# A hybrid attention block in float32: conv projections from unnormed rows, attention moved behind them, norm steps on VectorE, joined weight splits

## The chip, the cores and the metric

The kernel runs on one core of a Trainium2 chip. The metric is the device time of one execution in microseconds. One execution was taken by the hardware profiler; the rows below are of that one. TensorE (PE) multiplies matrices and loads its stationary operand beside that (PEld); VectorE (DVE), ScalarE (ACT) and GpSimd (POOL) work on elements; SyncE (SP) starts most DMA transfers.

## The reference

A layer with four token mixers side by side, merged by gates, and a feed-forward part, for 512 tokens of 1024 channels:

```python
# x: 1 x 512 x 1024, float32; one layer
h = rms_norm(x, attn_norm)                       # x * rsqrt(mean(x^2) + 1e-6) * gain
proj = einsum('bsd,dc->bsc', h, w_in)            # split into 17 parts:
(fq, fk, fv, ff, cu, cb, cc, mq, mk, mv, mi, mf, mo, sq, sk, sv, gates) = split(proj)

fq, fk = rms_norm(fq per head, fox_q_gain), rms_norm(fk per head, fox_k_gain)
# forget-gate attention, 4 heads of 64, causal, softmax over
#   q.k/8 + c_q - c_k   with c = cumsum(log_sigmoid(ff + bias))
y_fox = fox_attention(fq, fk, fv, ff + fox_f_bias)

def short_conv_mixer(u, b_gate, c_gate, w):
    z = c_gate * u
    y = conv over 3 positions of the sequence, one weight per channel and tap
    return b_gate * y
y_conv = short_conv_mixer(cu, cb, cc, conv_w)    # 256 channels

y_mlstm = sigmoid(mo) * rms_norm(mlstm(mq, mk, mv, mi, mf), mlstm_h_gain)
y_swa = swa_attention(rms_norm(sq), rms_norm(sk), sv, sinks, bias)   # 8 heads, window 128

g = sigmoid(gates)                               # 4 x 1024
merged = (g0 * (y_fox @ w_fox_out) + g1 * (y_conv @ w_conv_out)
        + g2 * (y_mlstm @ w_mlstm_out) + g3 * (y_swa @ w_swa_out))
x = x + merged @ w_merge_out
h = rms_norm(x, ffn_norm)
x = x + (silu(h @ w_gate) * (h @ w_up)) @ w_down      # 1024 -> 2816 -> 1024
```

## The kernel before

Everything lies transposed: channels on the 128 partitions, the 512 tokens along a row, so x is eight blocks of 128 x 512. TensorE works on a rounded float type (F32R); so each float32 operand is split into a high half, a cast made by ScalarE, and a low half, the difference, made by VectorE (`split`, lines 132 to 134; `scaled_split`, 136 to 139, with a factor per channel). A product is three matmuls in `mm3`: high with high (line 128), high with low and low with high.

**Weights** stream in through SP's queue in 139 pieces of 512 KB, each 1024 columns wide. `w_split` (line 160) splits half a piece, 512 columns, at a time; `w_take` hands them out and keeps `w_ahead` (5) halves split ahead; `w_raw` (3) pieces and `w_buf` (9) split halves have buffers.

**Start** (from line 222). For each of the eight blocks xc: the product with the channel gain is split into xh and xl (the list `xg`, rows that the norm has not touched), a token-major projection of 396 columns runs (psn, with weights wnr split into wnh, wnl of 396 columns each), and the squares go into `ssq`, added on GpSimd (line 243). From ssq come `rcol` and `rb_` (r = 1/sqrt(mean + eps), one value per token, spread over all partitions by a matmul with ones, pv_a), and `epsv`.

**Projections.** `proj` (line 394) multiplies eight blocks with two weight halves: 24 matmuls of 128 x 512. pfk and pfq (two each) use xg, since a norm per head follows them. The conv's pcu, pcc and pcb (two each), and every gate and projection behind them, use `xn`: `normed_input` (line 384) loads a block of x again as xs, multiplies it with rb_ on GpSimd (line 387) and splits it into xnh, xnl.

**Norm per head** (`head_normed`, `sum_split`, `head_normed_rest`, lines 438 to 465): ScalarE squares the projection, the square is split into u (cast on VectorE, line 447) and w (difference, on GpSimd, line 448), a matmul with `blk` sums over the head, VectorE and ScalarE make the inverse root (`rsqrt`, 141 to 146), GpSimd multiplies (line 464), then `k_stack` or `q_stack` split the result. It serves fk and fq (each twice), sk and sq0 to sq3.

**The conv** (lines 689 to 706): z = pcc x pcu, two shifted additions, times pcb, split into ych, ycl. **The gates** (`gated`, line 711): for each of eight output blocks d a projection of 24 matmuls with xn (gconv0 to gconv7), then the branch's out-projection (oconv), tanh on ScalarE, and VectorE multiplies and adds up.

**Order.** Each mm3 of a projection calls `tick()`. It counts down work that was put off by `later(steps, ...)`; each `period` ticks, if nothing is put off, it lets one step of a background generator run. Such generators are `fox_attention` (22 steps), `swa_attention` and `ml_attention`. `gate_rows` (line 310), in five steps, makes the gate rows, writes them to memory and reads four of them back, spread over all partitions, as negc (line 305, ScalarE's queue), for fox_attention's scores. `flush()` runs all that is left. In program order fox_attention begins when the first pcc is done, and is flushed behind `gated("conv")`; then come psk and psq0 to psq3, then `gated("fox")`. The framework's scheduler may then move an instruction ahead of others on its engine.

Of the kernel before, what the change touches and what calls it, by code (L numbers as in the profile page):

```python
# [8 lines left out]
F32 = mybir.dt.float32  # L9
# [7 lines left out]
P = 128  # L17
# [20 lines left out]
    "n_s": 58, "n_wk": 11, "w_raw": 3, "w_buf": 9, "w_ahead": 5, "mm": 4,  # L38
    "norm_lag": 18, "fox_p": 6, "fox_t": 4, "fox_v": 6, "swa_p": 10, "swa_t": 3, "swa_v": 5, "swa_d": 0,
    "ml_p": 4, "ml_v": 3, "ml_n": 8, "warm": 7, "xn_0": 3, "xn_p": 3,  # L40
# [4 lines left out]
def kernel(  # L45
# [114 lines left out]
    def w_split():  # L160
        i = stream["split"]
        if i >= 2 * n_w:
            return
        stream["split"] = i + 1
        while stream["raw"] <= min(i // 2 + W_RAW - 1, n_w - 1):
            w_load()
        raw = stream["raws"][i // 2][:, (i % 2) * NT:(i % 2) * NT + NT]
        hi = big.tile([P, NT], F32R, tag="whi", name=f"wh{i}", bufs=W_BUF)
        lo = big.tile([P, NT], F32R, tag="wlo", name=f"wl{i}", bufs=W_BUF)
        split(hi, lo, raw)  # L170
        stream["ready"].append((hi, lo))

    def w_take():
        while len(stream["ready"]) <= W_AHEAD and stream["split"] < 2 * n_w:
            w_split()
        return stream["ready"].pop(0)
# [7 lines left out]
    pace = {"period": 4, "count": 0}  # L184
# [12 lines left out]
    def tick():  # L197
        for d in deferred:
            d[0] -= 1
        due = [d for d in deferred if d[0] <= 0]  # L200
        for d in due:
            deferred.remove(d)
            d[1]()
        pace["count"] += 1
        if pace["count"] >= pace["period"] and not deferred:
            pace["count"] = 0
            bg()
# [19 lines left out]
    for ko in range(KO):  # L227
# [4 lines left out]
        wh = big.tile([P, NV], F32R, tag="whi", name=f"wnh{ko}", bufs=W_BUF)  # L232
        wl = big.tile([P, NV], F32R, tag="wlo", name=f"wnl{ko}", bufs=W_BUF)
        split(wh, wl, wr[ko // 2][:, (ko % 2) * NV:(ko % 2) * NV + NV])
# [3 lines left out]
        if ko == 0:  # L238
            nc.scalar.activation(ssq, xc[ko], AF.Square)
        else:  # L240
            sq = wk(f"xsq{ko}")
            nc.scalar.activation(sq, xc[ko], AF.Square)
            nc.gpsimd.tensor_tensor(ssq, ssq, sq, op=ALU.add)

    rb_ = s_tile("r_b")
    epsv = s_tile("epsv")
    rcol = const.tile([P, NB], F32, name="rcol")
# [21 lines left out]
    norm_rows(ssq, rb_, epsv, "a")  # L269

# [37 lines left out]
    def gate_rows():  # L308
# [19 lines left out]
        for hh in range(FOX_H):  # L328
            negc.append(bcast_row(f"negc{hh}", hh))
# [54 lines left out]
    def normed_input(ko):  # L384
        t = wk(f"xs{ko}")
        nc.sync.dma_start(t, xT[ko * P:(ko + 1) * P, :])
        nc.gpsimd.tensor_tensor(t, t, rb_, op=ALU.mult)
        h, l = s_tile(f"xnh{ko}", F32R), s_tile(f"xnl{ko}", F32R)
        scaled_split(h, l, t, col[:, C_AN + ko:C_AN + ko + 1])
# [55 lines left out]
    def sum_split(name, sq):  # L445
        h, l = s_tile(f"{name}u", F32R), s_tile(f"{name}w", F32R)
        nc.vector.tensor_copy(h, sq)
        nc.gpsimd.tensor_tensor(l, sq, h.bitcast(F32), op=ALU.subtract)
        return h, l
# [5 lines left out]
    def head_normed_rest(name, qg, sq, s2, eps, then):  # L455
# [8 lines left out]
        nc.gpsimd.tensor_tensor(qg, qg, sq, op=ALU.mult)  # L464
# [17 lines left out]
    def fox_attention():  # L482
        prob, trans, outs, sums = {}, {}, {}, {}

# [191 lines left out]
    for n in (6, 14, 22, 30, 38):  # L676
        later(n, lambda: next(gr, None))
    later(40, lambda: next(bl, None))
# [9 lines left out]
    for p in range(2):  # L688
        ps = proj(f"pcu{p}")
        u = wk(f"cu{p}")  # L690
        nc.scalar.copy(u, ps)
        ps = proj(f"pcc{p}")
        z = wk(f"cz{p}")
        nc.vector.tensor_tensor(z, ps, u, op=ALU.mult)
        if p == 0:
            pace["period"] = TUNE["fox_p"]
            background.append(fox_attention())
# [4 lines left out]
        ps = proj(f"pcb{p}")  # L702
# [36 lines left out]

    gated("conv", False)  # L740
    flush()
# [9 lines left out]

    gated("fox", False, TUNE["swa_p"], swa_attention)
# [207 lines left out]
```

## Time and profile before

| | before |
|---|---|
| median of 3 runs (lowest, highest) | 863.8 us (862.32, 864.12) |
| the profiled execution, and its span | 862.88 us, 861.1 us |
| TensorE busy, matmuls | 846.6 us (98%), x3879 |
| VectorE busy | 493.4 us (57%), x899 |
| ScalarE busy | 386.1 us (45%), x733 |
| GpSimd busy | 144.9 us (17%), x134 |
| mean DMA rate over the span | 101 GB/s |

Busy time is the time in which an engine worked on an instruction, as a share of the span. A matmul that follows another overlaps with it, so a row's duration (0.39 us) is longer than the distance between two starts (0.23 us). The granted clock (PEclk) is TensorE's clock as a share of full speed, 1.00 being 2.4 GHz.

### The profile page before, as it was taken

The numbers are of one execution on the slowest core, as the hardware profiler recorded it, in microseconds if no ns is written. First come the engines' busy times: TensorE is split into PE (matmuls) and PEld (weight loads), VectorE is DVE, ScalarE is ACT, GpSimd is POOL, SyncE is SP. The second block draws the span as 40 slices with busy tenths as digits, with TensorE's granted clock in tenths as the row PEclk, the third lists the DMA queues.
The fourth block names the chain that finished last, engine by engine and source line by source line (L and its number), as shares of the span: only waits on it lengthen the run. The fifth ranks groups of instructions, "written<-read, shape, count | busy, mean of one in ns | idle before, by whom it ended". The sixth has DMA issues, their size and how long they took to land.

```text
span 861.1 us, 10668 instructions
## 1 busy us (share of the span) xinstructions
PE 846.6 (98%) x3879; PEld 699.6 (81%) x3879; DVE 493.4 (57%) x899; ACT 386.1 (45%) x733; POOL 144.9 (17%) x134
## 2 busy tenths in 40 slices
PE   7999999999999999999999999999999999999998
PEld 6877788888788888888888888888888888888886
DVE  6899966459888886675745545444444333522320
ACT  7565555467665654554534444333333322322210
POOL 5262100024312001221211202111111111000000
PEclk9998999999999999999999999999999999999999
DMA  6642222242221522222224423222222232233310
GB/s 232 214 136 97 87 74 74 96 125 73 74 74 50 172 83 88 75 74 98 98 98 141 150 78 120 94 99 89 97 94 96 97 99 97 97 123 110 123 37 24
DMA packets 28520, 87.35 MB, mean 101 GB/s; under 512 B 3455, under 2 KB 5032, under 8 KB 28468
## 3 DMA queue, kind: packets, MB, share of 16 engines
q1 hardware_dynamic: 24716, 80.87, 27.6%
q10 hardware_dynamic: 3752, 5.81, 2.3%
q8 instruction: 30, 0.49, 0.2%
q14 instruction: 22, 0.18, 0.1%
HBM read 84.53 MB, written 2.13 MB: 101 GB/s over the span
## 4 chain that ended last, share of the span: by engine, by line
PE 84%; DVE 8%; ACT 3%; issue 2%; DMA 2%; SPq 0%; POOL 0%; DVEq 0%; ACTq 0%; POOLq 0%
PE dn L130 5%; PE fu L128 5%; PE dn L129 5%; PE fg L128 5%; PE fu L130 5%; PE fg L130 5%; PE fu L129 5%; PE fg L129 5%; PE dn L128 5%; PE gswa L129 2%; PE gswa L128 2%; PE gswa L130 2%; PE gmlstm L128 2%; PE gmlstm L130 2%; PE mg L130 2%
## 5 line engine op out<-in xcount | busy, mean ns | idle before, releaser
L134 DVE TENSOR_TENSOR wl<-wr,wh 128x512 fp32r<-128x512 f32 x278 | 203.0, 733 | 154.9 <-ACT wh L133 153.6
L133 ACT CAST wh<-wr 128x512 fp32r<-128x512 f32 x278 | 170.4, 619 | 262.7 <-PE dn L129 69.1
L823 POOL TENSOR_TENSOR ut<-ut,gt 128x512 f32<-128x512 f32 x22 | 34.2, 1554 | 204.8 <-DVE ut L822 166.6
L129 PE MATMUL fu<-x2l,wh 128*128 128x512 f32 x176 | 68.5, 389 | 0.0
L128 PE MATMUL fu<-x2h,wh 128*128 128x512 f32 x176 | 68.5, 389 | 0.0
L130 PE MATMUL fg<-x2h,wl 128*128 128x512 f32 x176 | 68.5, 389 | 0.0
L130 PE MATMUL fu<-x2h,wl 128*128 128x512 f32 x176 | 68.5, 389 | 0.0
L128 PE MATMUL fg<-x2h,wh 128*128 128x512 f32 x176 | 68.5, 389 | 0.0
L129 PE MATMUL fg<-x2l,wh 128*128 128x512 f32 x176 | 68.5, 389 | 0.0
L128 PE MATMUL dn<-ah,wh 128*128 128x512 f32 x176 | 68.5, 389 | 0.0
L129 PE MATMUL dn<-al,wh 128*128 128x512 f32 x176 | 68.5, 389 | 0.0
L130 PE MATMUL dn<-ah,wl 128*128 128x512 f32 x176 | 68.5, 389 | 0.0
L130 PEld LDWEIGHTS fg<-x2h,wl 128*128 128x128 f32 x176 | 33.1, 188 | 6.9
L129 PEld LDWEIGHTS fu<-x2l,wh 128*128 128x128 f32 x176 | 33.1, 188 | 6.9
L128 PEld LDWEIGHTS dn<-ah,wh 128*128 128x128 f32 x176 | 33.0, 188 | 6.9
L129 PEld LDWEIGHTS dn<-al,wh 128*128 128x128 f32 x176 | 33.0, 188 | 6.9
L129 PEld LDWEIGHTS fg<-x2l,wh 128*128 128x128 f32 x176 | 33.0, 188 | 6.9
L128 PEld LDWEIGHTS fu<-x2h,wh 128*128 128x128 f32 x176 | 33.1, 188 | 6.8
L130 PEld LDWEIGHTS fu<-x2h,wl 128*128 128x128 f32 x176 | 33.0, 187 | 6.9
L130 PEld LDWEIGHTS dn<-ah,wl 128*128 128x128 f32 x176 | 33.0, 188 | 6.7
L128 PEld LDWEIGHTS fg<-x2h,wh 128*128 128x128 f32 x176 | 33.0, 188 | 6.7
L822 DVE TENSOR_TENSOR ut<-fu,r 128x512 f32<-128x512 f32 x22 | 15.2, 691 | 29.9 <-PE fu L130 29.9
(598 smaller groups left out, 1930.7 us busy)
## 6 DMA issues: line engine op xcount, KB each, us to landing
wr<-in_w_str_dram SPq DMA_DIRECT2D x139, 512.0 KB, 3.3
xc<-in_xT_dram SPq DMA_DIRECT2D x8, 256.0 KB, 5.5
xs<-in_xT_dram SPq DMA_DIRECT2D x8, 256.0 KB, 4.0
xr<-in_xT_dram ACTq DMA_DIRECT2D x8, 256.0 KB, 2.6
out_dram<-o SPq DMA_DIRECT2D x7, 256.0 KB, 2.1
wnr<-in_w_tok_dram SPq DMA_DIRECT2D x3, 396.0 KB, 5.6
negc<-d_rows ACTq DMA_DIRECT2D x4, 256.0 KB, 5.7
bw<-d_line ACTq DMA_DIRECT2D x4, 256.0 KB, 3.7
```

What stands on the lines that cost most here:

```text
L128: nc.tensor.matmul(out, a[0], b[0], start=start, stop=False)
L129: nc.tensor.matmul(out, a[0], b[1], start=False, stop=False)
L130: nc.tensor.matmul(out, a[1], b[0], start=False, stop=stop)
L133: nc.scalar.copy(hi, src)
L134: nc.vector.tensor_tensor(lo, src, hi.bitcast(F32), op=ALU.subtract)
L822: nc.vector.tensor_tensor(ut, pu, r2, op=ALU.mult)
L823: nc.gpsimd.tensor_tensor(ut, ut, gt, op=ALU.mult)
```

## The change

- **Weights** are split 1024 columns at a time, one cast and one subtraction for a whole piece: 139 splits in place of 278. There are 4 buffers of 1024 columns for each half in place of 9 of 512, 4 in place of 3 raw pieces, and the look-ahead is 4 halves. At the start, pairs of 396 columns are split together (792), but for the first pair.
- **From GpSimd to VectorE** go the seven additions into ssq, the low halves in `sum_split`, the multiplication in `head_normed_rest`, and the one in `normed_input`, which now also takes the channel gain in, so that a plain split follows.
- **The conv projections** use xg. Since pcu and pcc are linear in the row, their product needs r twice: ScalarE makes r_sq = r x r, VectorE multiplies pcu by it in place of ScalarE's copy, and multiplies the conv's result with rb_ ahead of the product with pcb.
- **Later steps.** The first `normed_input` runs at tick 26, then one each 6 ticks (3 and 3 before); gate_rows at 8, 18, 28, 40, 50 (6 to 38 before).
- **fox_attention** is put into the background behind the conv projections and a flush, with period 5 (6 before), and runs on through psk and psq, where put-off work no longer holds it back (`mixed`). The negc loads stand at its beginning. A flush stands ahead of `gated("fox")`.

```diff
--- before.py
+++ after.py
@@ -35,9 +35,9 @@
 
 
 TUNE = {
-    "n_s": 58, "n_wk": 11, "w_raw": 3, "w_buf": 9, "w_ahead": 5, "mm": 4,
-    "norm_lag": 18, "fox_p": 6, "fox_t": 4, "fox_v": 6, "swa_p": 10, "swa_t": 3, "swa_v": 5, "swa_d": 0,
-    "ml_p": 4, "ml_v": 3, "ml_n": 8, "warm": 7, "xn_0": 3, "xn_p": 3,
+    "n_s": 58, "n_wk": 11, "w_raw": 4, "w_buf": 4, "w_ahead": 4, "mm": 4,
+    "norm_lag": 18, "fox_p": 5, "fox_t": 4, "fox_v": 6, "swa_p": 10, "swa_t": 3, "swa_v": 5, "swa_d": 0,
+    "ml_p": 4, "ml_v": 3, "ml_n": 8, "warm": 7, "xn_0": 26, "xn_p": 6,
 }
 
 
@@ -159,19 +159,19 @@
 
     def w_split():
         i = stream["split"]
-        if i >= 2 * n_w:
+        if i >= n_w:
             return
         stream["split"] = i + 1
-        while stream["raw"] <= min(i // 2 + W_RAW - 1, n_w - 1):
+        while stream["raw"] <= min(i + W_RAW - 1, n_w - 1):
             w_load()
-        raw = stream["raws"][i // 2][:, (i % 2) * NT:(i % 2) * NT + NT]
-        hi = big.tile([P, NT], F32R, tag="whi", name=f"wh{i}", bufs=W_BUF)
-        lo = big.tile([P, NT], F32R, tag="wlo", name=f"wl{i}", bufs=W_BUF)
-        split(hi, lo, raw)
-        stream["ready"].append((hi, lo))
+        hi = big.tile([P, 2 * NT], F32R, tag="whi", name=f"wh{i}", bufs=W_BUF)
+        lo = big.tile([P, 2 * NT], F32R, tag="wlo", name=f"wl{i}", bufs=W_BUF)
+        split(hi, lo, stream["raws"][i])
+        for h in (slice(0, NT), slice(NT, 2 * NT)):
+            stream["ready"].append((hi[:, h], lo[:, h]))
 
     def w_take():
-        while len(stream["ready"]) <= W_AHEAD and stream["split"] < 2 * n_w:
+        while len(stream["ready"]) <= W_AHEAD and stream["split"] < n_w:
             w_split()
         return stream["ready"].pop(0)
 
@@ -181,7 +181,7 @@
 
 
     background, deferred = [], []
-    pace = {"period": 4, "count": 0}
+    pace = {"period": 4, "count": 0, "mixed": False}
 
     def later(steps, fn):
         deferred.append([steps, fn])
@@ -202,7 +202,7 @@
             deferred.remove(d)
             d[1]()
         pace["count"] += 1
-        if pace["count"] >= pace["period"] and not deferred:
+        if pace["count"] >= pace["period"] and (pace["mixed"] or not deferred):
             pace["count"] = 0
             bg()
 
@@ -229,9 +229,15 @@
         xh, xl = s_tile(f"xh{ko}", F32R), s_tile(f"xl{ko}", F32R)
         scaled_split(xh, xl, xc[ko], g)
         xg.append((xh, xl))
-        wh = big.tile([P, NV], F32R, tag="whi", name=f"wnh{ko}", bufs=W_BUF)
-        wl = big.tile([P, NV], F32R, tag="wlo", name=f"wnl{ko}", bufs=W_BUF)
-        split(wh, wl, wr[ko // 2][:, (ko % 2) * NV:(ko % 2) * NV + NV])
+        half = slice((ko % 2) * NV, (ko % 2) * NV + NV)
+        if ko % 2 == 0:
+            wnh = big.tile([P, 2 * NV], F32R, tag="whi", name=f"wnh{ko}", bufs=W_BUF)
+            wnl = big.tile([P, 2 * NV], F32R, tag="wlo", name=f"wnl{ko}", bufs=W_BUF)
+            if ko:
+                split(wnh, wnl, wr[ko // 2])
+        if ko < 2:
+            split(wnh[:, half], wnl[:, half], wr[0][:, half])
+        wh, wl = wnh[:, half], wnl[:, half]
         for t in range(NB):
             tb = slice(t * P, (t + 1) * P)
             mm3(ps_n[t][:, 0:NV], (xh[:, tb], xl[:, tb]), (wh, wl), ko == 0, ko == KO - 1)
@@ -240,10 +246,11 @@
         else:
             sq = wk(f"xsq{ko}")
             nc.scalar.activation(sq, xc[ko], AF.Square)
-            nc.gpsimd.tensor_tensor(ssq, ssq, sq, op=ALU.add)
+            nc.vector.tensor_tensor(ssq, ssq, sq, op=ALU.add)
 
     rb_ = s_tile("r_b")
     epsv = s_tile("epsv")
+    r_sq = s_tile("r_sq")
     rcol = const.tile([P, NB], F32, name="rcol")
 
     def norm_rows(ssq, r_out, epsv_out, tag):
@@ -267,6 +274,7 @@
     nc.vector.tensor_scalar(vc, pcv[:, :, 0], 1.0 / D, EPS, op0=ALU.mult, op1=ALU.add)
     rsqrt(vc, rcol, yc, tcl)
     norm_rows(ssq, rb_, epsv, "a")
+    nc.scalar.activation(r_sq, rb_, AF.Square)
 
     snk = const.tile([P, SWA_H], F32, name="snk")
     nc.sync.dma_start(snk, bass.AP(sinks.tensor, sinks.offset, [[0, P], [1, SWA_H]]))
@@ -325,8 +333,6 @@
         nc.vector.tensor_tensor_scan(c[0:64], on[0:64], a[0:64], 0.0, op0=ALU.mult, op1=ALU.add)
         nc.vector.tensor_scalar(a[0:4], c[0:4], -1.0, None, op0=ALU.mult)
         nc.scalar.dma_start(d_rows[0:4], a[0:4])
-        for hh in range(FOX_H):
-            negc.append(bcast_row(f"negc{hh}", hh))
         yield
         ai = wk("g_ai")
         nc.gpsimd.memset(ai[0:64], 0.0)
@@ -384,9 +390,10 @@
     def normed_input(ko):
         t = wk(f"xs{ko}")
         nc.sync.dma_start(t, xT[ko * P:(ko + 1) * P, :])
-        nc.gpsimd.tensor_tensor(t, t, rb_, op=ALU.mult)
+        nc.vector.scalar_tensor_tensor(
+            t, t, col[:, C_AN + ko:C_AN + ko + 1], rb_, op0=ALU.mult, op1=ALU.mult)
         h, l = s_tile(f"xnh{ko}", F32R), s_tile(f"xnl{ko}", F32R)
-        scaled_split(h, l, t, col[:, C_AN + ko:C_AN + ko + 1])
+        split(h, l, t)
         xn.append((h, l))
 
 
@@ -445,7 +452,7 @@
     def sum_split(name, sq):
         h, l = s_tile(f"{name}u", F32R), s_tile(f"{name}w", F32R)
         nc.vector.tensor_copy(h, sq)
-        nc.gpsimd.tensor_tensor(l, sq, h.bitcast(F32), op=ALU.subtract)
+        nc.vector.tensor_tensor(l, sq, h.bitcast(F32), op=ALU.subtract)
         return h, l
 
     def head_sums(pm, s2):
@@ -461,7 +468,7 @@
         else:
             nc.vector.scalar_tensor_tensor(v, pm, 1.0 / HD, eps, op0=ALU.mult, op1=ALU.add)
         rsqrt(v, sq, y0, sq)
-        nc.gpsimd.tensor_tensor(qg, qg, sq, op=ALU.mult)
+        nc.vector.tensor_tensor(qg, qg, sq, op=ALU.mult)
         then(qg)
 
 
@@ -481,6 +488,8 @@
 
     def fox_attention():
         prob, trans, outs, sums = {}, {}, {}, {}
+        for hh in range(FOX_H):
+            negc.append(bcast_row(f"negc{hh}", hh))
 
         def scores(h, qt):
             q2, (ka, kb) = fq[h // 2][h % 2], fk[h // 2][h % 2]
@@ -673,9 +682,9 @@
     y["fox"], y["conv"], y["swa"], y["mlstm"] = [], [], [], []
     fq, fk, sq_, sk, mq, mk, mo, vm = [], [], [], [], [], [], [], []
     gr, bl = gate_rows(), swa_bias_line()
-    for n in (6, 14, 22, 30, 38):
+    for n in (8, 18, 28, 40, 50):
         later(n, lambda: next(gr, None))
-    later(40, lambda: next(bl, None))
+    later(56, lambda: next(bl, None))
     for ko in range(KO):
         later(TUNE["xn_0"] + TUNE["xn_p"] * ko, lambda ko=ko: normed_input(ko))
     for p in range(2):
@@ -686,20 +695,19 @@
 
 
     for p in range(2):
-        ps = proj(f"pcu{p}")
+
+        ps = proj(f"pcu{p}", xg)
         u = wk(f"cu{p}")
-        nc.scalar.copy(u, ps)
-        ps = proj(f"pcc{p}")
+        nc.vector.tensor_tensor(u, ps, r_sq, op=ALU.mult)
+        ps = proj(f"pcc{p}", xg)
         z = wk(f"cz{p}")
         nc.vector.tensor_tensor(z, ps, u, op=ALU.mult)
-        if p == 0:
-            pace["period"] = TUNE["fox_p"]
-            background.append(fox_attention())
         cw = [col[:, C_CW + 2 * k + p:C_CW + 2 * k + p + 1] for k in range(3)]
         nc.scalar.activation(u, z, AF.Copy, scale=cw[2])
         nc.vector.scalar_tensor_tensor(u[:, 1:], z[:, :-1], cw[1], u[:, 1:], op0=ALU.mult, op1=ALU.add)
         nc.vector.scalar_tensor_tensor(u[:, 2:], z[:, :-2], cw[0], u[:, 2:], op0=ALU.mult, op1=ALU.add)
-        ps = proj(f"pcb{p}")
+        nc.vector.tensor_tensor(u, u, rb_, op=ALU.mult)
+        ps = proj(f"pcb{p}", xg)
         nc.vector.tensor_tensor(u, ps, u, op=ALU.mult)
         yh, yl = s_tile(f"ych{p}", F32R), s_tile(f"ycl{p}", F32R)
         split(yh, yl, u)
@@ -737,8 +745,11 @@
                 pace["period"] = period
                 background.append(then())
 
+    flush()
+    pace["period"] = TUNE["fox_p"]
+    background.append(fox_attention())
     gated("conv", False)
-    flush()
+    pace["mixed"] = True
 
 
     swa_bias_load()
@@ -749,6 +760,8 @@
         ps = proj(f"psq{p}")
         head_normed(f"sq{p}", ps, qgain[:, 1:2], None, lambda q, p=p: sq_.append(q_stack(f"sq{p}", q, falling=True)))
 
+    pace["mixed"] = False
+    flush()
     gated("fox", False, TUNE["swa_p"], swa_attention)
```

The order on each engine, with the numbers of the program's buffers. First VectorE in the start, where the low halves xl of the input blocks stand among weight splits. Before:

```order
L134 TENSOR_TENSOR wnl_252<-wnr_84,wnh_251 128x396
L138 SCALAR_TENSOR_TENSOR xl_225<-xc_82,col,xh_224 128x512
L134 TENSOR_TENSOR wnl_275<-wnr_90,wnh_274 128x396
L134 TENSOR_TENSOR wnl_298<-wnr_90,wnh_297 128x396
L138 SCALAR_TENSOR_TENSOR xl_248<-xc_86,col,xh_247 128x512
```

and after:

```order
L138 SCALAR_TENSOR_TENSOR xl_219<-xc_82,col,xh_218 128x512
L249 TENSOR_TENSOR ssq<-ssq,xsq_257 128x512
L134 TENSOR_TENSOR wnl_265<-wnr_90,wnh_264 128x792
L249 TENSOR_TENSOR ssq<-ssq,xsq_280 128x512
L138 SCALAR_TENSOR_TENSOR xl_242<-xc_86,col,xh_241 128x512
L249 TENSOR_TENSOR ssq<-ssq,xsq_299 128x512
```

The sums into ssq have come between, and two splits have become one. xl_248 before and xl_242 after are the low half of the sixth block.

Second, VectorE and the normed blocks. Before, these stand ahead of the second step of the norm per head of the first projection:

```order
L138 SCALAR_TENSOR_TENSOR xnl_438<-xs_434,col,xnh_437 128x512
L138 SCALAR_TENSOR_TENSOR xnl_460<-xs_456,col,xnh_459 128x512
L138 SCALAR_TENSOR_TENSOR vs_364<-psn_133,rcol,vs_364 128x2x64
L295 TENSOR_SCALAR gc<-psn_133,rcol 128x3x4
L134 TENSOR_TENSOR wl_711<-wr_508,wh_710 128x512
L447 CAST fk0u<-fk0s 128x512
L138 SCALAR_TENSOR_TENSOR xnl_489<-xs_485,col,xnh_488 128x512
```

After, they stand behind the conv's and the second head norms' rows, up to the last one ahead of the attention:

```order
L134 TENSOR_TENSOR xnl_724<-xs_720,xnh_723 128x512
L134 TENSOR_TENSOR xnl_768<-xs_764,xnh_767 128x512
L441 CAST fk1b_703<-fk1b_703 64x512
L707 SCALAR_TENSOR_TENSOR cu_862<-cz_902,col,cu_862 128x511
L441 CAST fk1b_709<-fk1b_709 64x512
L471 TENSOR_TENSOR fq1g<-fq1g,fq1s 128x512
L708 SCALAR_TENSOR_TENSOR cu_862<-cz_902,col,cu_862 128x510
L709 TENSOR_TENSOR cu_862<-cu_862,r_b 128x512
L134 TENSOR_TENSOR fq1q_783<-fq1g,fq1q_783 64x512
L134 TENSOR_TENSOR fq1q_786<-fq1g,fq1q_786 64x512
L711 TENSOR_TENSOR cu_862<-pcb_908,cu_862 128x512
L134 TENSOR_TENSOR xnl_816<-xs_812,xnh_815 128x512
```

xnl_724, 768 and 816 are the fourth to sixth normed block; before, the first three are the ones shown, and the fourth followed two rows later. xnl_853 and xnl_887, the last two, follow behind the conv's ycl_821.

Third, TensorE at the first two gates, after:

```order
L130 MATMUL gconv_950<-xnh_723,wl_868 128x512
L128 MATMUL gconv_950<-xnh_767,wh_911 128x512
L129 MATMUL gconv_950<-xnl_768,wh_911 128x512
L130 MATMUL gconv_950<-xnh_767,wl_912 128x512
L128 MATMUL gconv_950<-xnh_815,wh_911 128x512
L128 MATMUL oconv_999<-ych_820,wh_867 128x512
L128 MATMUL gconv_1020<-xnh_536,wh_911 128x512
```

where before the first gate ran through its eight blocks at once:

```order
L130 MATMUL gconv_1095<-xnh_533,wl_994 128x512
L128 MATMUL gconv_1095<-xnh_562,wh_993 128x512
L129 MATMUL gconv_1095<-xnl_563,wh_993 128x512
```

After, the second gate (gconv_1020) begins with the first gate's last blocks still to come.

## Rows read from the trace of the kernel before

**Rows 1.** Windows: start:end, length, busy us (instructions) of each engine, clock, DMA.

```profile
core 0: us, PE busy (x) PEld busy (x) DVE busy (x) ACT busy (x) POOL busy (x), PEclk, DMA share, GB/s
18.77:21.53 2.76, 0.35 (x3) 0.02 (x2) 2.76 (x3) 2.20 (x4) 2.60 (x3) 1.00 0.24 58
21.53:28.63 7.10, 7.10 (x33) 7.05 (x34) 7.10 (x12) 2.38 (x5) 1.44 (x2) 0.76 0.57 196
...
58.00:70.00 12.00, 10.94 (x32) 6.23 (x31) 11.72 (x19) 6.58 (x13) 2.95 (x3) 0.72 0.40 132
70.00:94.87 24.87, 24.87 (x115) 20.31 (x114) 24.36 (x36) 14.97 (x27) 7.15 (x5) 1.00 0.19 66
94.87:111.00 16.13, 15.04 (x72) 12.00 (x71) 15.59 (x42) 10.35 (x25) 0.17 (x1) 1.00 0.29 98
111.00:176.00 65.00, 65.00 (x323) 53.33 (x322) 36.76 (x86) 32.80 (x68) 0.00 (x0) 1.00 0.27 91
176.00:232.00 56.00, 53.79 (x245) 43.79 (x244) 43.55 (x75) 37.93 (x69) 19.48 (x13) 1.00 0.25 84
...
400.00:600.00 200.00, 200.00 (x883) 165.54 (x882) 98.44 (x144) 84.13 (x135) 37.64 (x26) 1.00 0.32 107
```

**Rows 2.** Timeline of TensorE, start: start, duration, instruction, tiles, [idle before <- releaser].

```profile
18.59 0.34 PE L128 MATMUL psn<-wnh,xh 128*128 128x396 f32 x1
18.77 0.34 PE L129 MATMUL psn<-wnl,xh 128*128 128x396 f32 x1
21.53 1.58 PE L130 MATMUL psn<-wnh,xl 128*128 128x396 f32 x4 [2.41 <-DVE xl L138]
...
26.06 0.95 PE L265 MATMUL pc<-ones,ssq 128*128 128x2 f32 x8
...
28.63 0.39 PE L128 MATMUL pfk<-xh,wh 128*128 128x512 f32 x1
```

**Rows 3.** Timeline of VectorE, start.

```profile
9.45 1.05 DVE L134 TENSOR_TENSOR wnl<-wnr,wnh 128x396 fp32r<-128x396 f32 x2
...
16.56 3.24 DVE L134 TENSOR_TENSOR wnl<-wnr,wnh 128x396 fp32r<-128x396 f32 x2
19.72 1.75 DVE L138 SCALAR_TENSOR_TENSOR xl<-xc,col,xh 128x512 fp32r<-128x512 f32 x1
```

**Rows 4.** Timeline of GpSimd, start.

```profile
16.05 6.55 POOL L243 TENSOR_TENSOR ssq<-ssq,xsq 128x512 f32<-128x512 f32 x4
```

**Rows 5.** Timeline of TensorE at the first conv projections.

```profile
60.38 0.50 PE L128 MATMUL pcu<-xnh,wh 128*128 128x512 f32 x1 [0.43 <-ACT xnh L137]
...
62.20 0.50 PE L129 MATMUL pcu<-xnl,wh 128*128 128x512 f32 x1 [0.57 <-DVE xnl L138]
```

**Rows 6.** Timeline of VectorE, from 28 to 90 us.

```profile
46.46 0.42 DVE L447 CAST fk0u<-fk0s 128x512 fp32r<-128x512 f32 x1
...
75.95 1.52 DVE L447 CAST fq1u<-fq1s 128x512 fp32r<-128x512 f32 x1
...
83.49 0.68 DVE L134 TENSOR_TENSOR wl<-wr,wh 128x512 fp32r<-128x512 f32 x1
84.09 0.69 DVE L145 SCALAR_TENSOR_TENSOR fk1s<-fk1s,fk1v 128x512 f32<-128x512 f32 x1
```

**Rows 7.** Timeline of ScalarE, ahead of the attention and in the psq projections.

```profile
95.07 1.26 ACT L133 CAST fq1q<-fq1g 64x512 fp32r<-64x512 f32 x2 [3.70 <-POOL fq1g L464]
...
224.42 1.26 ACT L417 CAST sq3q<-sq3g 64x512 fp32r<-64x512 f32 x2 [3.37 <-POOL sq3g L464]
```

**Rows 8.** Timeline of TensorE, the first gate's first and the second gate's last matmul.

```profile
94.87 0.39 PE L128 MATMUL gconv<-xnh,wh 128*128 128x512 f32 x1
...
111.87 0.40 PE L130 MATMUL oconv<-ych,wl 128*128 128x512 f32 x1
```

**Rows 9.** Groups of GpSimd by shape: busy us, mean ns, idle before, releaser.

```profile
L464 POOL TENSOR_TENSOR sq3g<-sq3g,sq3s 128x512 f32<-128x512 f32 x1 | 1.6, 1608 | 1.3 <-DVE sq3s L146 1.3
```

**Rows 10.** The tile negc: time of its transfers.

```profile
DMA to landing us min/median/max: 5.5/5.7/6.0
```

## The prediction

> **What bounds the kernel now.** I read the windows first [rows 1]. From 111 to 176 us and through the second half TensorE is busy for the whole of a stretch at full clock: 883 matmuls in 200 us, 0.227 us each. The number of matmuls is not changed, so only time in which TensorE stands or runs at the lower clock can be won or lost: four places before 232 us. From 18.77 it is busy for 0.35 of 2.76 us, then runs 7.10 us at a granted clock of 0.76; from 58 to 70 it issues 32 matmuls in 12 us at 0.72; from 94.87 to 111 it stands 1.1 us; from 176 to 232, 2.2 us. VectorE is busy for 11.72 us of 58 to 70 and 24.36 of the next 24.87: there it feeds TensorE and is full. Behind 280 us nothing is to be had: in 400 to 600 VectorE is busy half the time and no matmul waits.
>
> Next the timeline, for what ends the waits. At 18.77 TensorE stops 2.41 us for the low half (xl) of the sixth input block [rows 2]. VectorE wrote it late because two weight splits beside GpSimd's sums of squares took 3.24 us, while two with GpSimd quiet took 1.05 [rows 3, 4]. At 60 and 62 us the conv projections wait for the normed blocks xnh and xnl [rows 5].
>
> **Part one, the start.** The seven sums go to VectorE, where an elementwise 512-column step with its issue takes 0.60 us (83.49 to 84.09) [rows 6]; a joined 792-column split lies between one 512-column step, 0.60, and two 396-column ones, 1.05 [rows 3]: I take 0.89, near the two, since columns grow by half. GpSimd then does no large step in this stretch, so I price VectorE at the quiet durations. From 9.85 (the cast of the first joined split is then done) up to the sixth xl stand three joined splits (2.7), six sums (3.6) and three xl (1.8), with 0.5 waiting for casts: 18.4. TensorE wants it at 18.95 (18.77 and a matmul's 0.18) [rows 2]: no wait, by half a microsecond. Then 24 matmuls of 0.183 (4.4), the eight column sums of squares (0.95 busy [rows 2]) and one 0.23 matmul come before the first projection, pfk: 24.5, against 28.63. **Start: 4.1 us won.** If the sixth or seventh xl is late after all, up to 2.4 of it goes, and the lower clock behind it comes back too; that is bounded by the same 4.1, and part three shows that it would not reach the end.
>
> **Part two, the projections.** The conv projections read xg, complete at the start. The stall of 58 to 70 goes: 32 matmuls need 7.3 us, so 4.7 of 12 is won. The gate stage begins with gconv at 94.87 [rows 8]; by these sums TensorE could begin it at 94.87 - 4.1 - 4.7 = 86.1. The scaling by r_sq and by r_b adds four VectorE steps of 0.60 and takes two copies off ScalarE.
>
> **Part three, the new wait.** The normed blocks are now needed by the first gate, and the order of VectorE puts the fourth, xnl_724, 15 rows before the last conv row and the last three right at the end. So VectorE's queue has to be summed. Its row fk0u stood at 46.46 [rows 6]; 4.1 earlier is 42.4. From there to the last row wanted (ycl_941) it has 86 rows: 8 splits of 1024 columns at 1.13 (9.0; bounds 0.60 for one 512-column step and 1.20 for two, so near the latter), 51 steps at 0.60 (30.6), 8 half-height ones at 0.65 (5.2), 13 casts at 0.38 (4.9), the gate rows 4.8, chained rows 2.0 (both by kind): 56.5, and 3.4 standing: 102. Row by row with each row's inputs it came to 100; I take 101. The fourth block is 15 rows, 8.7 us, earlier: 92. On ScalarE xnh_815 stands behind the two fq1q casts, which wait for VectorE's fq1g; before, these took 1.26 behind a wait of 3.70 [rows 7]. That puts xnh_815 and ych_820 at about 96.5. TensorE has by then issued 15 of the 60 matmuls of gates 0 and 1; 45 remain, 10.2 us: 106.7, and 1.1 for a spell at the lower clock and for the first tanh: 107.8.
>
> Before, both gates were done at 111.87 + 0.23 = 112.1 [rows 8]. That stretch of 17.2 us held 1.1 idle and 13.6 of gate matmuls, so 2.5 us of attention work, which now comes later: the like-for-like point is 109.6. **So of the 8.8 us won by 86, 7.0 are given back and 1.8 stay.** Since VectorE sets this point, a start that wins a microsecond more or less changes it only by what VectorE's queue gets of it.
>
> What VectorE pays for the moved work: up to here 7 sums, 4 low halves, 4 multiplies by the norm and 5 of the 8 first norm steps, 20 steps at 0.60 = 12 us. What it gets: the cast beside GpSimd's subtraction took 1.52, alone 0.42 [rows 6]; such rows, with the start's, add to 9 or 10 us, and each joined split saves up to 0.07 against two. That nearly balances, hence no large gain.
>
> Here a rule bears. By the rows, VectorE slows down only while GpSimd reads. The Trainium skill, "SBUF — State Buffer", Who interferes with whom, says that a VectorE instruction with two SBUF inputs contends with a GpSimd instruction that reads SBUF; the rows of 16.56 agree. The Trainium skill, "Perfetto Trace Analysis", Optimizing Scalar/DVE Operations, says that offloading between these two might not help; that one is weighed as a rival.
>
> **Part four, the attention moved and the joined splits.** fox_attention's steps and its four negc loads on ScalarE's queue now stand behind ych_940. A negc load took 5.7 us to land [rows 10], so from some 98 it lands by 103.5; TensorE has gates until 107.8: nothing waits. The steps then run in 111 to 176, where no matmul waits, and end beside the psk and psq projections. Behind 111 the weight splits are covered by TensorE's work, so joining them is worth nothing there; uncovered, the cost would be half a joined split, 0.5 us, once for each wait.
>
> In 176 to 232 the chains of the four psq heads end on GpSimd's multiply (ScalarE waits 3.37 us for sq3g [rows 7]). On VectorE that multiply takes 0.60 for 1.61 us [rows 9], and the low half likewise; with two such links saved I keep 0.5 of the 2.2 idle: **1.7 won** (bounds 0 and 2.2). But attention rows now share VectorE there (43.55 of 56 busy); they may cost the gain, not more than that.
>
> **Sum.** 1.8 + 1.7 = 3.5. The profiled execution took 862.9 us (span 861.1, and 1.8 around it), so 859.4; the median shown is 0.9 above it: 863.8 - 3.5 = **860.3**.
>
> **Rivals.** (a) VectorE's wait eats the start's gain whole: its 86 rows come 2 to 3 us dearer than summed (all splits at 1.20 and 5 standing), so gates 0 and 1 end at 110 and only 176 to 232 wins: 862.1 to 865.5, no change that can be told. For it: VectorE is busy for 24.36 of 24.87 us at that place today. Against: it counts on relief that is smaller than the rows show. (b) VectorE arrives 4 us earlier: at 97, because its quiet steps overlap and the idle 3.4 goes; TensorE ends the two gates at 103.8, and 5.8 + 1.7 = 7.5 are won: **856.3**. For it: before, such rows ran at 0.60 with hardly a gap. (c) **Slower, by the clock.** Two waits of 6 and 3 us at gate 0 stand in one place; today the clock fell to 0.76 behind a wait of 2.41 and to 0.72 in the stall of 58 to 70. At 0.76 over 7.10 us a spell costs 1.7, at 0.72 over 12 it costs 3.4. Two spells of the longer kind at gates 0 and 1 cost 6.8 where I set 0.6: 860.3 + 6.2 = 866.5. It decides from a cost of about 6 us. Against: the clock was 1.00 in the 94.87 stretch with its 1.1 idle. (d) **Slower: the relief doesn't come.** Then VectorE carries the 12 us of moved steps in full; the place at gate 0 moves from 101 to about 110, TensorE from 107.8 to 117, and 863.8 + 7.4 - 1.7 (or 0) is 869.5 to 871; with half of it, 864.9. Against: cast 0.42 and 1.52, splits 1.05 and 3.24 [rows 3, 6]. The Trainium skill's "Perfetto Trace Analysis" would, by its sentence on offloading, end here. (e) The change not doing what it says: the scheduler moves the norms late by itself; that is (a).
>
> **Chances.** Forecast 0.45 (858.5 to 862), (b) 0.21, (a) with (e) 0.21, (c) 0.08, (d) 0.05. About 0.2% (1.7 us) is what a measurement of this kernel can tell from no change. Faster 0.66, same 0.21, slower 0.13. The range that leaves out no more than 2 in 10 reaches from under (b), 854.5, to the upper end of (a) with half of (c), 866.
>
> **What would show it.** After: pfk begins at 24 to 25.5 and the clock stays 1.00 until there; pcu to pcb run without a wait and end by 87; a wait of TensorE at gconv for xnl (fourth block) of 5 to 8 us, and a second for xnh or ych of up to 4; VectorE busy without a gap from 42 to 100; gates 0 and 1 done at 107 to 109; negc not waited for; less than 1 us of idle time in the stage of psk and psq. I am wrong if gate 0 runs through by 90 without a wait (then b), if the clock is under 0.8 for more than 6 us behind 85 (c), or if VectorE's 512-column steps take over 0.65 with GpSimd quiet (d).

## The result

The changed kernel takes 870.43 us (869.23 to 870.82, 6 runs), the kernel before 863.56 (862.32 to 864.53) beside it: 1.0077, 95% interval 1.0066 to 1.0088. I had forecast 860.3 and a range of 854.5 to 866: **slower by 6.9 us where 3.5 us faster was forecast**, outside the range. The profiled execution took 869.23 us, its span 867.4.

The windows of the profile after, cut as in [rows 1] (start:end, length, busy us and instructions of each engine, granted clock, DMA):

```profile
18.77:21.53 2.76, 2.53 (x16) 2.29 (x14) 2.76 (x5) 2.76 (x4) 0.31 (x1) 1.00 0.63 205
21.53:28.63 7.10, 7.10 (x40) 6.44 (x39) 4.34 (x9) 0.92 (x4) 0.52 (x1) 1.00 0.68 220
...
58.00:70.00 12.00, 12.00 (x56) 9.70 (x55) 11.63 (x19) 4.43 (x7) 0.00 (x0) 1.00 0.32 108
70.00:94.87 24.87, 18.92 (x85) 14.36 (x84) 24.48 (x38) 12.93 (x19) 0.00 (x0) 0.96 0.34 109
94.87:111.00 16.13, 13.69 (x48) 10.45 (x48) 11.65 (x24) 7.89 (x15) 0.00 (x0) 0.74 0.27 96
...
176.00:232.00 56.00, 51.94 (x234) 42.77 (x233) 45.56 (x89) 36.76 (x70) 4.27 (x3) 0.97 0.23 76
232.00:280.00 48.00, 48.00 (x289) 42.58 (x288) 36.55 (x117) 26.83 (x74) 8.53 (x13) 1.00 0.24 77
280.00:400.00 120.00, 117.88 (x554) 98.32 (x553) 80.19 (x146) 59.88 (x107) 15.11 (x22) 0.99 0.29 89
400.00:600.00 200.00, 200.00 (x883) 165.15 (x881) 104.22 (x115) 78.67 (x101) 42.58 (x25) 1.00 0.33 108
```

Against [rows 1] the first two places are mended: TensorE issues 16 matmuls, not 3, from 18.77 to 21.53, and 40 at full clock in the next stretch; 58 to 70 has 56 matmuls where it had 32. Three places lose more than that: 70 to 111 with 8.4 us of idle time and a clock of 0.74 in its second part; 176 to 232 with 4.06 us idle; and 280 to 400, where before no matmul waited, with 2.12. Behind 400 nothing has changed: 883 matmuls in 200 us. The kernel before, in the two stretches that [rows 1] leaves out:

```profile
232.00:280.00 48.00, 46.97 (x286) 41.32 (x285) 40.12 (x131) 28.18 (x86) 9.48 (x13) 1.00 0.20 67
280.00:400.00 120.00, 120.00 (x562) 99.93 (x561) 89.76 (x174) 65.41 (x132) 18.05 (x25) 1.00 0.30 100
```

TensorE's five longest waits (us in total, times, longest):

```profile
PE gconv L129 <- DVE xnl L134: 6.0, 1, 6.0
PE ss L567 <- DVE sq2q L425: 2.5, 1, 2.5
PE gconv L128 <- ACT xnh L133: 2.4, 1, 2.4
PE gswa L128 <- ACT tswa L733: 2.1, 1, 2.1
PE gfox L128 <- ACT tfox L733: 1.6, 1, 1.6
```

**The start** went by the sum. Timeline of TensorE (start, duration, instruction, idle before and releaser), beside [rows 2]:

```profile
18.68 0.34 PE L129 MATMUL psn<-wnl,xh 128*128 128x396 f32 x1
19.25 0.98 PE L130 MATMUL psn<-wnh,xl 128*128 128x396 f32 x4 [0.23 <-DVE xl L138]
...
24.79 0.40 PE L128 MATMUL pfk<-xh,wh 128*128 128x512 f32 x1
```

The wait of 2.41 us is 0.23, and pfk begins at 24.79 (28.63 before, 24.5 forecast).

**The first gate.** Timeline of TensorE, 85 to 103 us:

```profile
85.92 0.47 PE L128 MATMUL gconv<-xnh,wh 128*128 128x512 f32 x1
...
88.08 0.40 PE L128 MATMUL gconv<-xnh,wh 128*128 128x512 f32 x1
94.43 0.79 PE L129 MATMUL gconv<-xnl,wh 128*128 128x512 f32 x1 [5.95 <-DVE xnl L134]
95.02 0.63 PE L130 MATMUL gconv<-xnh,wl 128*128 128x512 f32 x1
...
99.37 0.79 PE L128 MATMUL gconv<-xnh,wh 128*128 128x512 f32 x1 [2.44 <-ACT xnh L133]
...
103.04 0.49 PE L128 MATMUL gconv<-xnh,wh 128*128 128x512 f32 x1
```

The gate begins at 85.92 (86.1 forecast), gets through three blocks and waits twice. Behind the waits most starts stand 0.43 us apart, not 0.23, until 103.04. What VectorE did meanwhile:

```profile
44.37 0.42 DVE L454 CAST fq0u<-fq0s 128x512 fp32r<-128x512 f32 x1
...
93.69 1.29 DVE L134 TENSOR_TENSOR xnl<-xs,xnh 128x512 fp32r<-128x512 f32 x2
...
103.25 0.69 DVE L134 TENSOR_TENSOR ycl<-cu,ych 128x512 fp32r<-128x512 f32 x1
```

From 44.37 (fq0u) to 103.94 are 59.6 us and 86 rows, which I had summed at 59.9 (56.5 and 3.4 standing). The length was right; it begins 2 us later than I had put it.

**The forget gates.** TensorE and then ScalarE, 212 to 217 us:

```profile
214.42 0.33 PE L567 MATMUL ss<-ska,sq2q 128*128 128x128 f32 x1 [2.50 <-DVE sq2q L425]
...
216.41 0.80 PE L128 MATMUL gfox<-xnh,wh 128*128 128x512 f32 x1 [1.56 <-ACT tfox L733]
```

```profile
212.54 1.26 ACT L424 CAST sq2q<-sq2g 64x512 fp32r<-64x512 f32 x2
213.82 0.63 ACT L143 ACTIVATE sq3y<-sq3s 128x512 f32<-128x512 f32 x1
214.47 1.28 ACT L733 ACT_TABLE_LOAD   x1
215.77 1.09 ACT L733 ACTIVATE tfox<-gfox 128x512 f32<-128x512 f32 x2
```

The scores of the sliding window (ss) stand on TensorE ahead of the next gate's matmuls, and the head norms that they need are not done; on ScalarE the tanh of the gates (tfox), with a table load of 1.28 us, stands behind those norms.

**The gates of the sliding window.** ScalarE, then TensorE, at 353 us:

```profile
353.18 1.04 ACT L133 CAST wh<-wr 128x1024 fp32r<-128x1024 f32 x1 [4.52 <-PE oswa L129]
354.33 0.63 ACT L659 ACTIVATE msq<-mh 128x512 f32<-128x512 f32 x1
354.87 1.07 ACT L733 ACTIVATE tswa<-gswa 128x512 f32<-128x512 f32 x2
```

```profile
355.50 0.53 PE L128 MATMUL gswa<-xnh,wh 128*128 128x512 f32 x1 [2.12 <-ACT tswa L733]
```

A joined cast waits 4.52 us for TensorE to finish with the weights whose buffer it takes; two tanh stand behind it, and TensorE waits for them.

### The profile page after: what moved, and what is told of

Read it like the earlier page. It is cut to its first block, busy times and chain, and to the rows that moved or that the text cites. A ratio compares the mean times of both kernels' runs of the same rounds, so it can differ in the third digit from the quotient of the medians.

```text
span 867.4 us, 10170 instructions
## 1 busy us (share of the span) xinstructions
PE 846.0 (98%) x3879; PEld 700.5 (81%) x3879; DVE 496.2 (57%) x796; ACT 359.7 (41%) x588; POOL 95.8 (11%) x99
## 4 chain that ended last, share of the span: by engine, by line
PE 59%; DVE 0%; DVEq 0%; issue 0%
PE fu L129 5%; PE dn L128 5%; PE fg L129 5%; PE dn L129 5%; PE fu L128 5%; PE fg L130 5%; PE fu L130 5%; PE fg L128 5%; PE dn L130 5%; PE gmlstm L128 2%; PE gmlstm L129 2%; PE mg L129 2%; PE mg L128 2%; PE gmlstm L130 2%; PE mg L130 2%; PE gswa L128 1%
## 5 line engine op out<-in xcount | busy, mean ns | idle before, releaser
L133 ACT CAST wh<-wr 128x1024 fp32r<-128x1024 f32 x139 | 146.0, 1050 | 287.4 <-issue 110.9
L134 DVE TENSOR_TENSOR wl<-wr,wh 128x1024 fp32r<-128x1024 f32 x139 | 189.7, 1365 | 107.1 <-ACT wh L133 106.4
```

The costliest lines, as they stand in the source:

```text
L133: nc.scalar.copy(hi, src)
L134: nc.vector.tensor_tensor(lo, src, hi.bitcast(F32), op=ALU.subtract)
```

## The experiments

Each kernel ran beside the kernel before on the same chip (863.2 to 863.4). Ratios are to that, with 95% intervals.

| kernel | edit, to the changed kernel unless said | us | ratio |
|---|---|---|---|
| u1_splits512 | 512-column splits | 867.67 | 1.0048 [1.0031, 1.0065] |
| u2_buf5 | five joined buffers | 869.83 | 1.0071 [1.0056, 1.0086] |
| u8_conv_xn | conv on normed rows, these early | 860.97 | 0.9967 [0.9954, 0.9980] |
| g2 | gates 0 and 1 on unnormed rows too | 862.46 | 0.9988 [0.9978, 0.9997] |
| u11_xn_early | normed blocks early | 864.50 | 1.0015 [1.0005, 1.0024] |
| u4_pool_norm | norm steps back on GpSimd | 870.38 | 1.0083 [1.0063, 1.0104] |
| u5_start_only | kernel before, seven sums on VectorE | 862.27 | 0.9985 [0.9976, 0.9994] |
| u6_noflush | no flush of norms ahead of the forget gates | 861.72 | 0.9975 [0.9964, 0.9985] |
| u12_early_noflush | u11 and u6 | 855.30 | 0.9917 [0.9892, 0.9942] |
| v1_convxn_noflush | u8 and u6 | 855.76 | 0.9913 [0.9898, 0.9928] |
| u14_512_noflush | u1 and u6 | 862.14 | 0.9984 [0.9974, 0.9993] |
| u7_fox_early | attention at its old place | 868.63 | 1.0058 [1.0038, 1.0079] |
| w1_before_flush | kernel before, flush added | 865.91 | 1.0030 [1.0018, 1.0042] |
| w2_fox_moved | kernel before, sums on VectorE and attention moved | 862.84 | 0.9991 [0.9981, 1.0000] |

**The last place: joined splits or buffers.** u1_splits512 has the old `w_split`; u2_buf5 this:

```diff
-    "n_s": 58, "n_wk": 11, "w_raw": 4, "w_buf": 4, "w_ahead": 4, "mm": 4,
+    "n_s": 56, "n_wk": 11, "w_raw": 3, "w_buf": 5, "w_ahead": 4, "mm": 4,
```

> The changed kernel with the weights split 512 columns at a time as before (3 raw pieces, 9 buffers, look-ahead 5; 396 columns at the start); all else of the change stays. Theory: a joined cast of 1024 columns waits on ScalarE's queue for a buffer (4.52 us at 353 us) while the tanh that TensorE needs stands behind it, so the 2.1 us wait of gswa and the slow matmuls behind it (4.2 us together) come from the joining: about 866.2, with no wait of gswa for tanh over 0.5 us; the waits at the first gate stay. Rival: that wait comes from where the changed order puts the mLSTM rows, not from the splits: about 870 and the wait stays.

> The changed kernel with 5 joined weight buffers instead of 4 (and 3 raw pieces instead of 4, 56 row tiles instead of 58, to make room); the splits stay joined. Theory: what the cast waits for at 353 us is a free buffer, so a fifth one takes the wait of gswa away: about 866.2. Rival: the length of a joined cast and subtraction (1.05 and 1.22 us) is what hurts, not the number of buffers: about 870 as the changed kernel.

With 512 columns the wait of gswa is gone: from the first gswa to the first gmlstm matmul are 77.5 us, where the changed kernel has 81.5. Of these 4 us 2.8 show in the time (the waits at the first gate grew from 8.4 to 9.4 us). With a fifth buffer everything stands as it was, the cast again 4.52 us late:

```profile
353.80 1.05 ACT L133 CAST wh<-wr 128x1024 fp32r<-128x1024 f32 x1 [4.52 <-PE oswa L129]
```

Counted in the traces, the cast that stands there is now that of the next piece, the 52nd and not the 51st: one more buffer moves the waiting cast one piece on, to the same place in the queue. I had expected the buffer to help. Why 512 columns do help, by the smaller piece or by the other buffers and look-ahead that come with it, is not shown.

**The first gate: what waits, and why.** u8_conv_xn undoes the unnormed projections, g2 extends them, u11_xn_early only makes the normed blocks early:

```diff
-    "ml_p": 4, "ml_v": 3, "ml_n": 8, "warm": 7, "xn_0": 26, "xn_p": 6,
+    "ml_p": 4, "ml_v": 3, "ml_n": 8, "warm": 7, "xn_0": 3, "xn_p": 3,
```

> The changed kernel with the conv projections on the normed rows as before, the normed blocks and gate rows at the early steps as before; norms on VectorE, attention behind the conv and joined splits stay. Theory: VectorE's queue is the limit up to the first gate, whatever stands in it first, and it loses 4 steps of 0.6 us: the two waits at gconv (6.0 and 2.4) go, a stall at pcu and pcc comes back, and the gates begin about 2.4 us earlier than in the changed kernel: 867 to 869. Rival: the unnormed projections alone make the first gate late, and without them the start's gain is kept whole: 862 to 864.

> The changed kernel, with the first two conv gates also taken from the unnormed rows (r_b put on their results on VectorE ahead of the tanh) and the normed blocks made only behind the conv projections (put-off steps 76, 78, ...; attention starts without the flush). Theory: TensorE's wait at the first gate is for the normed blocks alone, which VectorE makes last; without that need the 6.0 and 2.4 us waits and the half-clock matmuls behind them go: 862 to 864.5. Rival: the conv's own rows (ycl) and the split weights come just as late, so half of it stays: 866 to 868.

> The changed kernel with only the put-off steps of the normed blocks as before (first at tick 3, then each 3); conv projections stay unnormed. It tells order from load. Order theory: TensorE waited at the first gate because VectorE had the normed blocks last, behind head norms that no one needed yet; with them first, both waits at gconv go and, since pcu needs no normed block, no stall comes in their place: 858 to 862. Load theory: VectorE's 58 us of work ahead of the first gate stays the same, so another late row (ych or ycl of the conv) takes the wait's place for 4 us or more: 865 to 868.

My theory of the load, that VectorE's 58 us of work come first whatever stands first in them, is wrong. u8 wins 9.5 us over the changed kernel where 1.4 to 3.4 were expected; some 4 of them are not won here, since the wait at gswa is missing in u8 too, but 5.5 stay. u11 wins 5.9. TensorE's waits in u11_xn_early that have to do with this stretch:

```profile
PE oconv L128 <- ACT ych L133: 2.0, 1, 2.0
...
PE pa L351 <- DVE g_ai L340: 1.0, 1, 1.0
PE pcc L128 <- DVE cu L701: 0.8, 1, 0.8
PE pcb L128 <- ACT fk1g L448: 0.7, 1, 0.7
```

Where 8.4 us had been waited at gconv, 2.0 are waited at oconv and 2.5 in three small places. The queue is as long as it was: the last ycl ends at 103.96 (103.94 in the changed kernel). But the last normed block, among the last rows at 102.04 there, is early in u11:

```profile
60.36 0.68 DVE L134 TENSOR_TENSOR xnl<-xs,xnh 128x512 fp32r<-128x512 f32 x1
```

What stands last now are head norms of the attention, which no gate needs, and the conv's own rows, for which oconv waits. The time of u11, between its two expectations, has the later waits still in it (tanh at gfox 3.8, gswa 2.1). g2 came out in the range of its first theory, but in part by luck. The waits for normed blocks are gone; 3.8 us of waits for tconv, the multiplication that the edit adds on VectorE, stand at the same gates; and the wait at gswa is gone as well. The attention's start without the flush of the blocks came with the edit, so g2 is less clean than u11.

**GpSimd or VectorE.**

> The changed kernel with the low halves of the head sums, the multiplications of the head norms and those of the normed blocks back on GpSimd (the seven sums of squares stay on VectorE). No-relief theory: VectorE is rid of some 16 steps of 0.6 us ahead of the first gate, so the two waits at gconv shrink by 5 us or more: 863 to 866. Relief theory: VectorE's rows beside GpSimd get longer by what it is rid of, and the chain through GpSimd is longer: 868 to 872.

870.38 against 870.43: sixteen steps fewer on VectorE ahead of the first gate change nothing in all, as the relief theory said. The windows of VectorE alone (busy us and rows, clock, DMA) from fk0u to the last ycl, in the changed kernel and then in u4, say how:

```profile
41.45:103.94 62.49, 59.09 (x92) 0.92 0.34 111
41.11:107.28 66.17, 59.68 (x76) 0.92 0.29 98
```

With 16 rows fewer VectorE is busy as long. The equal time hides two shifts: the wait at gconv is 7.5 us for 8.4, and the waits at the forget gates are 5.7 for 4.1.

**The start alone.**

```diff
-            nc.gpsimd.tensor_tensor(ssq, ssq, sq, op=ALU.add)
+            nc.vector.tensor_tensor(ssq, ssq, sq, op=ALU.add)
```

> The kernel before with one edit: the seven additions of the sum of squares on VectorE. If the start's 4.1 us is kept to the end: 859 to 860. If VectorE's queue gives it back at the conv projections (the stall of 58 to 70 grows by it): 862.5 to 863.5.

862.27: of some 4 us, 1.1 stay. TensorE now gets to the conv projections early and waits there:

```profile
55.03 0.79 PE L128 MATMUL pcu<-xnh,wh 128*128 128x512 f32 x1 [3.28 <-ACT xnh L137]
```

**The flush.** u6_noflush takes away one call:

```diff
     pace["mixed"] = False
-    flush()
+    while background:
+        bg()
     gated("fox", False, TUNE["swa_p"], swa_attention)
```

> The changed kernel without the flush of put-off head norms ahead of the forget gates (the attention alone is finished there). If the flush puts the scores of the sliding window ahead of norms that are not done (2.5 us for sq2q, 1.6 us for tanh, and half-clock matmuls, 5.9 us in all around 212 us): 865 to 867. If what stands there is the table load and VectorE's rows of the psq norms, as before the change (3.4 us in 200 to 240, 1.8 in 240 to 280): 869.5 to 871.

861.72: **8.7 us of the changed kernel hang on this one line.** In its windows both late places are nearly whole:

```profile
200.00:232.00 32.00, 31.49 (x149) 25.77 (x148) 28.85 (x56) 24.09 (x40) 4.50 (x3) 1.00 0.20 66
...
340.00:360.00 20.00, 20.00 (x91) 16.44 (x90) 12.94 (x17) 8.01 (x10) 3.91 (x2) 1.00 0.27 87
```

where the changed kernel has

```profile
200.00:232.00 32.00, 27.94 (x125) 23.03 (x124) 27.29 (x61) 20.17 (x43) 4.27 (x3) 0.95 0.20 66
...
340.00:360.00 20.00, 17.88 (x75) 14.34 (x74) 12.47 (x17) 6.94 (x11) 4.48 (x4) 0.91 0.25 79
```

Without the flush the head norms of sq2 and sq3 are put off into the first gates, and since put-off work holds the background back, the scores come behind them. On TensorE of u6_noflush the scores for sq2 stand seven microseconds later, behind gates, and wait for nothing:

```profile
221.69 0.22 PE L567 MATMUL ss<-ska,sq2q 128*128 128x128 f32 x1
```

The table load alone is not to blame: one of 1.28 us stands at 210.36 on ScalarE in u6 as well. And the idle time of 200 to 232 is 0.51 us in u6 where it was 2.21 before the change: the 1.7 us forecast for the psq chains are won once the flush is gone.

> The kernel before with one line added: the flush of the put-off head norms ahead of the forget gates. If the flush costs by itself, by putting the scores of the sliding window and the norms of the last two heads ahead of the gates' matmuls: 3 us or more over the kernel before, 866.5 to 870, with a wait for sq2q or tanh around 210 us. If it hurts only with what the change does beside it (the attention through psk and psq, joined splits): 863 to 864.5.

In the kernel before, the same line costs 2.5 us, between what the two theories said. The waits are the same ones:

```profile
PE ss L558 <- DVE sq2q L418: 2.5, 1, 2.5
PE gfox L128 <- ACT tfox L725: 2.1, 1, 2.1
```

There it only adds to a place that lost 2.2 us already, and gswa does not wait. So the flush's own price is 2.5 us there and between 4 and 5 in the changed kernel (8.7 less some 4 at gswa). The wait at gswa comes on top only with joined splits, and not always with them: u8 and g2 keep joined splits and the flush and do not have it. In u6 the joined cast stands behind the two tanh on ScalarE, where the changed kernel has it ahead of them:

```profile
348.85 1.07 ACT L733 ACTIVATE tswa<-gswa 128x512 f32<-128x512 f32 x2
349.80 1.06 ACT L133 CAST wh<-wr 128x1024 fp32r<-128x1024 f32 x1
```

It does so in u8 and g2 as well (349.26 behind 348.31, 349.80 behind 347.83). TensorE's wait goes with the cast's place in ScalarE's queue; why the scheduler gives the one place or the other is not settled.

**Two edits together, and the parts alone.**

> The changed kernel with both single edits: normed blocks made early (first at tick 3, then each 3) and no flush of the put-off head norms ahead of the forget gates. If the two losses are separate, the gains add (5.9 and 8.7 us): 855 to 857. If the early blocks only move VectorE's late rows, or if the second loss comes from the phase in which the stage is reached: 860 or more.

> The changed kernel with the conv projections on the normed rows, early norms and gate rows as before, and without that flush. If the flush is a loss of its own, as with the changed kernel (5.9 us around 207 us, the gswa wait being absent here already): 855 to 857. If the flush hurt only behind a late conv: 860 to 861.

> The changed kernel without that flush and with the weights split 512 columns at a time. Beside the changed kernel without the flush (861.7) it gives the price of the joined splits where no gswa wait exists. If joining hurts only through that wait: 861 to 862.5. If each joined split delays TensorE elsewhere: 858 to 860.

The losses are separate and the gains add: **855.30 and 855.76, 0.8 to 0.9% under the kernel before.** One has unnormed conv projections, the other normed ones, so these are worth nothing of their own that the runs can tell. The width of the splits is worth nothing either once the flush is gone (861.72 and 862.14).

> The changed kernel with the attention at its old place (background from the first pcc, period 6, flushed behind the conv gates, negc loads early), and so without the flush ahead of the forget gates as well; unnormed conv projections, late normed blocks, norms on VectorE and joined splits stay. Beside the changed kernel without that flush (861.7) it gives the price of the attention's place. If VectorE is the limit ahead of the first gate, attention rows there make it later: 864 to 868. If they fill waiting time: 860 to 862.

> The kernel before with two parts of the change: the seven sums on VectorE, and the attention put behind the conv projections and run on through psk and psq, without the flush of the put-off norms (normed conv projections, head norms and normed blocks on GpSimd, 512-column splits as before; one extra square on ScalarE is left in). If these two carry what the version at 855.8 wins over the kernel before: 855 to 858. If the head norms on VectorE or the joined splits carry a part: 859 to 862.

u7 took 868.63 with the very waits of the changed kernel at the first gate (5.8 and 2.4): the attention's place decides nothing there, and my reason for a loss was wrong. It loses in 200 to 232 (28.20 us busy, clock 0.89), having psk and psq without the attention beside them; how far that and how far the order of the norms is to blame was not taken apart. w2 says the same from the other side: start and attention moved, without the norms on VectorE and joined splits, give no difference (862.84), where with them 855.76 was measured. Its waits are at the normed blocks that pass through GpSimd:

```profile
PE pcu L128 <- ACT xnh L137: 3.1, 1, 3.1
...
PE pcu L129 <- DVE xnl L138: 1.1, 1, 1.1
```

Since the splits' width does nothing by itself where the normed blocks are late (u14), the norms on VectorE are the likely source of most of the 7.1 us between w2 and v1; the two were not separated, so that is not shown.

## Why the prediction was wrong

- **The start** was right: 3.8 us for 4.1, pfk at 24.79 for 24.5. That VectorE's queue gives most of it back was right as well; u5 keeps 1.1.
- **The projections**: no wait, gate at 85.92 for 86.1. Right.
- **The wait at the first gate** was foreseen by place and cause, and its size missed by 3.7 us: 1.8 were to be won there, but the first gfox matmul, ahead of which both kernels have the conv gates and the attention, starts 1.9 us later than before (196.3 for 194.4). Two terms of the sum were mis-sized. First the anchor: the 86 rows reach from fq0u to the last ycl, but were set on the time of fk0u, five rows earlier (from there it is 91); fq0u began at 44.37, not 42.4, so the fourth block came at 94.4 for 92 and xnh at 99.3 for 96.5. Second the clock: 0.6 us was put down; from 99.37 to 103.04 eight steps took 3.67 us where 1.82 were due, 1.85 lost. So the sign of rival (c), the clock under 0.8 for more than 6 us, came (0.74 over 94.87 to 111), but part of the slow spell was hidden by the second wait, and the loss beyond the 0.6 was 1.25 us, not 6.2.
- **GpSimd's work on VectorE** "nearly balances": right at that place (u4). Rival (d), that relief fails, fell: VectorE took 59.6 us where 59.9 were summed. The Trainium skill, "Perfetto Trace Analysis", Optimizing Scalar/DVE Operations, says that offloading between VectorE and GpSimd might not help. u4 agrees: 870.38 and 870.43. But w2 beside v1 is a case where the chain through GpSimd is probably what TensorE waits for.
- **176 to 232** was forecast to win 1.7 and lost 1.9 of idle time there, and with 232 to 280, where the 1.0 idle went, 0.8. From the first gfox to the first gmlstm matmul are 209.2 us (196.3 to 405.5) where 204.9 were (194.4 to 399.3); some 4 of the 4.3 belong to gswa, so by this measure 0.3 was lost at the forget gates, 2.0 less than forecast. The step that failed is part four: I listed the flush ahead of the forget gates in the change and gave it no price. I shortened the chains of the psq norms by their durations, which u6 bears out, and did not ask when they are called for. The flush calls the scores before the norms are done.
- **280 to 400** was priced at nothing: "Behind 111 the weight splits are covered by TensorE's work". A split is covered; what stands behind it in ScalarE's queue is not. The Trainium skill, "Perfetto Trace Analysis", Optimizing Scalar/DVE Operations, says that breaking up instructions may allow work to be completed sooner where an engine that isn't full makes bubbles on others. u1 agrees: 2.12 us of waiting gone with half the width. I had put "0.5 us, once for each wait" and no place.

Together: 3.7 at the first gate, some 2 at the forget gates and some 4 at gswa make 9.7 of the 9.8 us by which the profiled execution missed (869.23 for 859.4; the medians are 10.1 apart). No rival named the two later places; the slower ones, (c) and (d), had other mechanisms.

## What to carry to other kernels

An engine that works through a full queue in order delays others by the order of its rows more than by their sum: ask for each row who waits for it, and put rows without a waiter last. A flush, a barrier or any "do it all now" in code that feeds a scheduler is an edit with a price of its own: here one line cost 8.7 us, where all the rest of the change won 1.6 (861.72 beside 863.32). And when an instruction that waits for a buffer is made larger, look at what stands behind it on its queue, and not only at whether it is covered itself.

## What was not expected of the hardware

The lower clock also costs behind the wait, and only some waits are followed by it. The 5.95 and 2.44 us at gconv were followed by 0.63 us matmuls up to 103.04, and the 2.12 us at gswa by a clock of 0.91 over 340 to 360. In u12_early_noflush TensorE waits 1.78 us at oconv, and the stretch around keeps its clock:

```profile
84.00:112.00 28.00, 26.22 (x124) 21.40 (x123) 22.78 (x43) 12.79 (x24) 0.00 (x0) 1.00 0.29 95
```

The length alone does not tell which: at the start a wait of 2.41 us in the kernel before was followed by a clock of 0.76 over 21.53 to 28.63, and one of 2.39 in w1_before_flush by 1.00 over the same stretch. So the waits of the changed kernel at gconv and gswa cost more than their length, which the sum of waits alone does not show.
